# A two-layer encoder trunk in three-part fp32: x's second form split sooner, five of a pair's low parts by DMA, the last way down's buffers in another order, and PSUM tiles of two banks

## The chip, the cores and the metric

The kernel runs on one core of a Trainium2 chip. The time of a run is device microseconds for one launch. The time before is the median of three runs; the trace comes from one further, profiled execution. PE is TensorE, DVE VectorE, ACT ScalarE, POOL GpSimd, SP the engine that issues most loads.

## The reference

512 tokens of width 1024 go through two layers. Each layer is feed-forward, mixer, feed-forward, and a gated layer input, each with a residual and a layer norm:

```python
for i in range(DEPTH):                                   # DEPTH = 2
    x = layer_norm(A * x + 0.5 * swiglu_ffn(x, ffn1_wgu[i], ffn1_wd[i]), ...)
    x = layer_norm(A * x + (mlstm_mixer if i == 0 else gmlp_mixer)(x, ...), ...)
    x = layer_norm(A * x + 0.5 * swiglu_ffn(x, ffn2_wgu[i], ffn2_wd[i]), ...)
    ple = sigmoid(x @ ple_wg[i] + ple_bg[i]) * (p[i] @ ple_wp[i])
    x = layer_norm(A * x + ple, ...)

def swiglu_ffn(x, w_gu, w_d):                            # 1024 -> 2 x 2816 -> 1024
    g, u = split(x @ w_gu, 2)
    return (silu(g) * u) @ w_d
```

All is float32. The change touches the four feed-forward stages, and the places where a mixer or the gated input takes PSUM banks.

## The kernel before, in words

**Numbers in two parts.** A float32 operand is split into a high part (`whi`, `xh`: a ScalarE copy, L242) and a low part (`wlo`, `xl`: the rest, a VectorE subtraction, L251 or L257). `mm3` (L351 to L355) makes three matmuls of each product: high by high (L353), low by high (L354), high by low (L355).

**Weights.** `Weights` is one ordered list of (buffer kind, loads, make). `fill` takes it strictly in order: an entry is split as soon as a buffer of its kind is free, and the entries behind it wait for it. Kinds are `main` (4 buffers), `rows` (2 in a feed-forward stage) and `rowsx` (1, opened in the last pair at r = 2). Raw weights come by SP into 3 raw slots (`wraw`, 1 MB each) or smaller `wquarter` tiles; a slot is free when the last part made from it is done. A low part can also be made "by DMA": ScalarE writes the raw block negated, and rounded as the high part is, into `wlo` (L248), and POOL issues a transfer that adds the raw block to it (L249).

**A feed-forward stage** goes through the hidden columns in chunks of 2, 4, 4, 4, 4 and 4 blocks of 128. Chunks 0 to 3 make plain up products (`fps`, 24 matmuls of 512 columns each). Chunks 4 and 5 make them in pairs: seven products (`ups`, r = 0 to 6, 24 matmuls of 256 columns) give the gate and up blocks of two column blocks at once, after Strassen's scheme. There are four such pairs in a stage, 16 in the kernel. Their operands are sums of weight blocks and of x's quarters:

- weights (`up_forms`, L127): a11, a12, s2, s1, s3, s4, a22 for r = 0 to 6; s2 is formed in place on VectorE at L141 and L142, s3 at L149 and L150. `UP_BY_DMA` lists the r whose low part goes by DMA.
- x (`UpForms`, L950): plain quarters for r = 0, 1, 5; the forms t2 (`t_whi`, `t_wlo`) for r = 2, t1 (`t`) for r = 3, t3 for r = 4, t4 (`t_f`) for r = 6. They are made in chunk 3: from its third product on, two entries of `steps` follow each product. What is left is in `last`, which runs an entry after a product s of chunk 4 (there s = r in the first pair).

A product's result is taken by `UpPair.take`: ScalarE copies the bank after r = 0, 2 and 3 (L1047, `us<-ups`), and VectorE adds the bank to the copy after r = 1, 4 and 5 (L1050, L1052); `gate` is the Silu (L1061). Product r = 4 writes the bank that r = 2 filled, so it must wait for that copy. In `up_products` the order after each product is: product, `group.add`, `take`, the form's low part, the waiting low parts of weights, `formed.last`, release and fill, `gate`, forms of coming weights, and after every odd s a product of the way down.

**The way down** of chunk c is made during chunk c + 1 by a `Group`: seven products (`gps`, 12 matmuls of 512 columns) after the same scheme. A product fills two PSUM banks, which stay pinned, and `add` adds them to the residual `xt` by two VectorE instructions of 128x512 (L727). The last chunk's way down is plain (`down`, `dps`): four token blocks of 128, each over four row blocks of `wd`, into two banks; block t = 1 needs the second pair of banks, which the last `gps` products held until their adds. The order of that way down's weight buffers is a list, one for stages A and C, one for B and D, which end with the gated input (`ple`).

**PSUM for this** is a pool `ps_dn` of four single banks, handed out in turn by `dn_bank`; `turn_x` (transposes of x, `xps`), the mixers (`gvps`, `gps`) and the gated input (`pwp`) take banks from it as well.

The stages are A (first layer, before the mixer mlstm), B (first layer, after it, with ple), C (second layer, before the mixer gmlp) and D (after it, with ple).

Of the kernel before, what the change touches and what calls it, by code (L numbers as in the profile page):

```python
# [10 lines left out]
F32 = mybir.dt.float32  # L11
# [31 lines left out]
W_BUFS = 4  # L43
EXTRA = 2
PLE_EXTRA = 3
UP_BY_DMA = (1, 4, 5, 6)


class Weights:
# [273 lines left out]
def hybrid_trunk(ctx: ExitStack, tc, x, p, ln_g, ln_b, ffn1_wgu, ffn1_wd, ffn2_wgu, ffn2_wd,  # L323
# [18 lines left out]
    tmp = side_pool("tmp", 4, "right")  # L342
    small = side_pool("small", 4, "right")
    ps_up = ctx.enter_context(tc.tile_pool(name="ps_up", bufs=1, space=PSUM))
    ps_dn = ctx.enter_context(tc.tile_pool(name="ps_dn", bufs=1, space=PSUM))
    dram = ctx.enter_context(tc.tile_pool(name="dram", bufs=1, space=DRAM))

    mm = nc.tensor.matmul
# [29 lines left out]
        up_order.remove(i)  # L378
        up_order.append(i)

    dn_order, pinned = deque(range(4)), {}

    def dn_bank(name, pin=False):

        i = next(i for i in dn_order if i not in pinned.values())
        dn_order.remove(i)
        dn_order.append(i)
        bank = ps_dn.tile([P, 512], F32, name=name, tag=f"dn{i}")
        if pin:
            pinned[id(bank)] = i  # L390
        return bank

    def unpin(bank):
        i = pinned.pop(id(bank))
        dn_order.remove(i)
        dn_order.append(i)

# [43 lines left out]
    def ffn_weights(wgu, wd, name, ple=False):  # L441
        starts = [sum(FFN_CHUNKS[:c]) for c in range(LAST + 1)]

        def forms(c):
            m = FFN_CHUNKS[c] // 2

            def quarter(i, j):
                k = starts[c] + m * i
                return kp(wd)[:, k:k + m, j * 512:(j + 1) * 512]
            loads = [W.add_load(quarter(i, j), n, name) for i, j, n in ((0, 0, 2), (0, 1, 1), (1, 1, 1), (1, 0, 2))]  # L450
            return W.forms("rows", *((j, slice(None)) for j in loads))

        first = len(W.order)
        for at in range(starts[UP_FROM]):
            if at == 0 or at == starts[UP_FROM] - 1:
                W.add(*((kp(wgu)[:, :, c0:c0 + P], [slice(None)]) for c0 in (at * P, HID + at * P)))
            elif at % 2:
                add_pairs(wgu, at * P, HID + at * P)
        tiles = W.order[first:]
        del W.order[first:]  # L460
        for c, n in enumerate(FFN_CHUNKS):
            down_w = deque(forms(c - 1) if c else ())
            if c >= UP_FROM:
                products = []
                for b in range(starts[c], starts[c] + n, 2):
                    products += W.up_forms(*(W.add_load(kp(wgu)[:, :, c0:c0 + 2 * P], 2) for c0 in (b * P, HID + b * P)))
                for s, product in enumerate(products):
                    W.order.append(product)
                    if s % 2:
                        W.order.append(down_w.popleft())  # L470
                continue
            for i in range(2 * n):
                W.order.append(tiles[2 * starts[c] + i])
                if down_w:
                    W.order.append(down_w.popleft())
        if ple:
            W.add_hook("rows", lambda hi, lo: turn_p.pop()(hi, lo))
        add_rows(wd, starts[LAST], 4, ["rows", "rowsx", "main", "main"] if ple else ["main", "rows", "rows", "rowsx"])


    ML_SLOTS = (2, 3, 4, 5, 6, 7, 11)
# [271 lines left out]
    def down(hs, first, norm=None, lazy=False, defer=False):  # L753


        n = len(hs)
        ws, kinds = [], []

        def release(k):
            kind = kinds[k] if kinds[k].startswith("rows") else None  # L760
            if norm is None:
                W.release(kind=kind)
            elif kind:
                W.free[kind] += 1
            elif defer:
                W.release()
            else:
                W.release(later=lazy or bool(W.held))
                if not W.held:
                    W.held.append("none")  # L770

        for t in range(TB):
            banks = [dn_bank("dps"), dn_bank("dps")]
            for k in range(n):
                if k == len(ws):
                    ws.append(W.take())
                    kinds.append(W.kind)
                if norm is not None and k == 1 and t:
                    norm.prepare(t - 1)
                    if t >= 2:  # L780
                        turn_x(t - 2, up_bank, (0,), norm)
                        if not norm.deferred:
                            turn_x(t - 2, up_bank, (1,), norm)
                    norm.scale(t - 1)
                if norm is not None and k == 2 and t >= 2 and norm.deferred:
                    turn_x(t - 2, up_bank, (1,), norm)
                st = [a[:, t * P:(t + 1) * P] for a in hs[k]]
                for half, ps in enumerate(banks):
                    mv = [a[:, 0, half * 512:(half + 1) * 512] for a in ws[k]]
                    mm3(ps, st, mv, k == 0, k == n - 1)  # L790
                if t == TB - 1:

                    if norm is None or k > 2:
                        release(k)
                    elif k == 2:
                        for j in range(3):
                            release(j)

            def finish(t=t, banks=banks):
                for half, ps in enumerate(banks):  # L800
                    residual(t, half, ps, first)
                    if norm is not None:
                        norm.stats(t, half, 2)
                if norm is not None and t == TB - 1:
                    norm.apply(t)
                    set_hooks(norm)

            if defer and t == TB - 1:
                return finish
            finish()  # L810
            if first:
                run_affine()
# [51 lines left out]
    class Group:  # L864
# [58 lines left out]
        def product(self):  # L923
# [3 lines left out]
                self.finish_form()  # L927
            w, f = W.take(), self.ready.popleft()
            if r < 2:
                self.banks.append([dn_bank("gps", True) for _ in range(2)])  # L930
            for e, ps in enumerate(self.banks[r % 2]):
                for k in range(self.half):
                    i, j = (e, k) if self.by_tokens else (k, e)
                    mm3(ps, [a[:, i, j * P:(j + 1) * P] for a in f], [a[:, k] for a in w],
# [2 lines left out]
        def add(self):  # L937
# [3 lines left out]
                return  # L941
            self.next_add += 1
            i, j = self.TO[r]
            for e, ps in enumerate(self.banks[r % 2]):
                residual(2 * i + e, j, ps, r in self.first)
                if r >= 5:
                    unpin(ps)


    class UpForms:  # L950


        def __init__(self, pool, late):

            f32 = lambda at, tag: at.tile([P, 4, 256], F32, name="x_" + tag, tag=tag)
            a = [tmp.tile([P, 2, 256], F32, name="x_a", tag="pad", bufs=3) for _ in range(2)]
            b, c = f32(late, "wlo"), f32(pool, "f0")
            both = act.tile([P, 2, 4, 256], F32R, name="t1", tag="gb")
            self.t1, self.t2, self.t4 = [both[:, 0], both[:, 1]], [], []
            self.t3 = self.quarter(0, 1)  # L960
# [21 lines left out]
            def split_t1():  # L982
                for i, s in enumerate(halves):
                    split(self.t1[0][:, s], self.t1[1][:, s], a[i])

            self.steps = [
                x22, lambda: joined(b, 0, 1), t3, lambda: joined(c, 0, 0), lambda: vec.tensor_add(c, b, c),
                lambda: sca.activation(f32r(self.t2, late, "whi"), c, AF.Copy), t1, split_t1]

            d = [tmp.tile([P, 2, 256], F32, name="x_d", tag="pad", bufs=3) for _ in range(2)]  # L990

# [2 lines left out]
                    joined(d[i], 1, 0, s)  # L994

            def t4():
                hi = f32r(self.t4, pool, "f1")
                for i, s in enumerate(halves):
                    vec.tensor_sub(d[i], d[i], c[:, s])
                    sca.activation(hi[:, s], d[i], AF.Copy)  # L1000

            def t3_t2():
                split(*self.t3, b)
                vec.tensor_sub(f32r(self.t2, late, "wlo"), c, self.t2[0].bitcast(F32))

            def t4_low():
                lo = f32r(self.t4, pool, "f0")
# [1 line left out]
                    vec.tensor_sub(lo[:, s], d[i], self.t4[0][:, s].bitcast(F32))  # L1009

            self.steps += [x21, t4]
            self.last = {0: t3_t2, 3: t4_low}
            self.right = [self.quarter(0, 0), self.quarter(1, 0), self.t2, self.t1, self.t3,
                          self.quarter(1, 1), self.t4]

# [55 lines left out]
    def ffn(layer, k, rows, late, prepare=None):  # L1071
        with stage_pool("forms", 2) as fpool, stage_pool("quarters", Q_BUFS) as qpool, \
# [51 lines left out]
                return next_group if h is not None else None  # L1124

            for c, n in enumerate(FFN_CHUNKS):
                if c < LAST:
                    h = hpool.tile([P, 4, SEQ], F32, name="h", tag="h")[:, :n]
                elif prepare is not None:
                    prepare()  # L1130
# [61 lines left out]
    def mlstm():  # L1192
        b_in = ml_b_in
        with stage_pool("extra", EXTRA) as extra, stage_pool("ml_parts") as near, stage_pool("forms", 2) as fpool, \
# [11 lines left out]
                return a.rearrange("p a b -> p (a b)")  # L1206

            def gate_products():
                ps = dn_bank("gps")
                for kb in range(KB):  # L1210
                    st = gw[:, kb].rearrange("p e c -> p (e c)")
# [332 lines left out]
    def gmlp():  # L1544
        with stage_pool("extra", EXTRA) as extra, stage_pool("gm_parts") as near, stage_pool("ghpool") as hpool, \
# [54 lines left out]
            for c in range(4):  # L1600
# [8 lines left out]
                for t in range(TB):  # L1609
                    if t:  # L1610
                        run_hook()
                    if t == 1 and c < 3:
                        next_vb = load_bias(c + 1)
                    ps = dn_bank("gvps")
                    up_tokens(t, ws, ps, hook=run_hook if t else None, release=give_back)
                    dst = v_cols(c * 512, 512)[:, t]
# [146 lines left out]
    def ffn_ple(i, last):  # L1763
        with stage_pool("rows", 2) as rows, stage_pool("late") as late:
# [20 lines left out]
            with stage_pool("extra", PLE_EXTRA) as extra, stage_pool("rows2") as rows2, stage_pool("ple2") as mp:  # L1785
                W.open("extra", extra, PLE_EXTRA)
                W.open("rows2", rows2, 1)
                W.fill(2)
                finish()
                ph, pl = ph[0], pl[0]  # L1790
                bg = mp.tile([P, D], F32, name="bgb")
                sca.dma_start(bg, row_ap(ple_bg, i * D, D))
# [66 lines left out]
    def warm(n):  # L1859

        ps = up_bank("warm")
        for _ in range(n):
            nc.tensor.transpose(ps[:, :P], ident, ident)

    warm(16)
    turn_x(0)
    turn_x(1)
# [12 lines left out]
    ffn_stage(1, 0)  # L1880
    gmlp()
    ffn_ple(1, True)


# [25 lines left out]
```

## Time and profile before

| | |
|---|---|
| median of 3 runs | 2246.17 us (2243.39 to 2249.09) |
| profiled execution, its own time | 2251.26 us |
| span of its trace | 2249.5 us |
| mean granted TensorE clock | 0.994 |
| PE busy | 2207.3 us, 11669 matmuls |
| VectorE busy | 1693.8 us, 2452 instructions |
| ScalarE busy | 1059.5 us, 1492 instructions |
| POOL busy | 159.0 us, 199 instructions |
| low parts by DMA (L249) | 112 issues of 512 KB |

In a timeline row the columns are start (us from the span's start), duration (us), engine, line, operation, out<-in, shape; "xN" joins N instructions in a row, and the brackets give the idle time ahead of it and what ended it. In a row of waits they are the total in us, how often, and the longest. Instructions of VectorE and ScalarE overlap slightly, so that the distance of two starts is a little less than a duration.

### The profile page before, as it was taken

How to read it: one execution, taken by the hardware profiler on the slowest of the kernel's cores; microseconds unless marked ns; L12 is line 12 of the kernel's file. 1: busy time of each engine (PE TensorE's matmuls, PEld its weight loads, DVE VectorE, ACT ScalarE, POOL GpSimd, SP SyncE). 2: the span in 40 equal slices, each digit the busy share in tenths (PEclk: the TensorE clock that was granted, in tenths of full speed). 3: DMA queues.
4: the chain of work that ended last, by engine and by line, in shares of the span. 5: the costliest groups of instructions: out<-in, count | busy, mean ns of one | idle time of the engine just before them, and what ended most of it. 6: DMA issues, size and time to landing. Idle time of an engine off the chain costs nothing. (4 is left out here: it accounts for less than half of the span.)

```text
span 2249.5 us, 29438 instructions
## 1 busy us (share of the span) xinstructions
PE 2207.3 (98%) x11669; PEld 1896.6 (84%) x11669; DVE 1693.8 (75%) x2452; ACT 1059.5 (47%) x1492; POOL 159.0 (7%) x199
## 2 busy tenths in 40 slices
PE   9999999999999999999999999999999999999998
PEld 8888987888888888888888888987888888888877
DVE  5668787786776776688786768886788767678887
ACT  4334655464646433356444334655345453336542
POOL 1000110111101100001000000110001100001000
PEclk9999999999999999999999999999999999999999
DMA  6323754456847443246532333754437733335551
GB/s 200 104 93 113 179 137 131 108 143 133 155 123 155 126 131 94 93 121 161 169 122 66 115 101 112 178 135 137 140 76 151 168 122 113 103 113 124 139 168 57
DMA packets 215538, 287.31 MB, mean 128 GB/s; under 512 B 6836, under 2 KB 161588, under 8 KB 215400
## 3 DMA queue, kind: packets, MB, share of 16 engines
q1 hardware_dynamic: 168080, 211.83, 29.2%
q0 software_dynamic: 40704, 58.91, 16.4%
q10 hardware_dynamic: 6616, 14.69, 2.0%
q8 instruction: 92, 1.51, 0.3%
q14 instruction: 46, 0.38, 0.1%
HBM read 224.58 MB, written 2.11 MB: 101 GB/s over the span
## 5 line engine op out<-in xcount | busy, mean ns | idle before, releaser
L242 ACT ACTIVATE whi<-wraw 128x1024 fp32r<-128x1024 f32 (+1 forms) x388 | 400.0, 1047 | 247.8 <-DVE wraw L142 90.8
L353 PE MATMUL fps<-xh,whi 128*128 128x512 f32 x800 | 311.4, 389 | 0.0
L354 PE MATMUL fps<-xl,whi 128*128 128x512 f32 x800 | 311.2, 389 | 0.0
L355 PE MATMUL fps<-xh,wlo 128*128 128x512 f32 x800 | 311.2, 389 | 0.0
L251 DVE TENSOR_TENSOR wlo<-wraw,whi 128x1024 fp32r<-128x1024 f32 (+1 forms) x214 | 257.0, 1216 | 52.5 <-ACT whi L242 51.9
L353 PE MATMUL gps<-whi,fhi 128*128 128x512 f32 x644 | 251.9, 391 | 0.0
L354 PE MATMUL gps<-wlo,fhi 128*128 128x512 f32 x644 | 251.6, 391 | 0.0
L355 PE MATMUL gps<-whi,flo 128*128 128x512 f32 x644 | 251.3, 390 | 0.0
L242 ACT ACTIVATE whi<-wquarter 128x1024 fp32r<-128x1024 f32 (+1 forms) x140 | 135.6, 969 | 201.0 <-PE gps L355 132.8
L249 POOL DMA_DIRECT2D wlo<-wraw x112 | 114.2, 1020 | 1500.5 <-ACT wlo L248 1309.6
L251 DVE TENSOR_TENSOR wlo<-wquarter,whi 128x1024 fp32r<-128x1024 f32 (+1 forms) x92 | 97.6, 1061 | 160.6 <-ACT whi L242 160.6
L727 DVE TENSOR_TENSOR xt<-xt,gps 128x512 f32<-128x512 f32 x302 | 193.0, 680 | 1.2 <-PE gps L355 1.2
L355 PEld LDWEIGHTS fps<-xh,wlo 128*128 128x128 f32 x800 | 150.2, 188 | 31.3
L353 PEld LDWEIGHTS fps<-xh,whi 128*128 128x128 f32 x800 | 150.2, 188 | 31.1
L354 PEld LDWEIGHTS fps<-xl,whi 128*128 128x128 f32 x800 | 150.2, 188 | 30.9
L353 PE MATMUL ups<-xh,whi 128*128 128x256 f32 x512 | 147.6, 288 | 12.2 <-ACT us L1047 12.2
L355 PE MATMUL ups<-xh,wlo 128*128 128x256 f32 x512 | 147.5, 288 | 1.1 <-DMA wlo<-wraw 1.1
L354 PE MATMUL ups<-xl,whi 128*128 128x256 f32 x512 | 146.1, 285 | 0.0
L355 PEld LDWEIGHTS gps<-whi,flo 128*128 128x128 f32 x644 | 120.9, 188 | 26.2
L353 PEld LDWEIGHTS gps<-whi,fhi 128*128 128x128 f32 x644 | 121.1, 188 | 23.9
L354 PEld LDWEIGHTS gps<-wlo,fhi 128*128 128x128 f32 x644 | 121.1, 188 | 23.6
L905 ACT ACTIVATE fhi<-h 128x512 fp32r<-128x512 f32 (+1 forms) x140 | 80.8, 577 | 120.2 <-DVE h L1151 50.4
(361 smaller groups left out, 5056.5 us busy)
## 6 DMA issues: line engine op xcount, KB each, us to landing
wraw<-in_ffn_wgu_dram SPq DMA_DIRECT2D x79, 1024.0 KB, 7.3
wlo<-wraw POOLq DMA_DIRECT2D x112, 512.0 KB, 5.9
wquarter<-in_ffn_wd_dram SPq DMA_DIRECT2D x64, 512.0 KB, 3.8
wraw<-in_ml_w_in_dram SPq DMA_DIRECT2D x24, 1024.0 KB, 5.8
wraw<-in_gm_w_in_dram SPq DMA_DIRECT2D x15, 1024.0 KB, 5.6
wraw<-in_ffn_wgu_dram SPq DMA_DIRECT2D x17, 512.0 KB, 4.9
wraw<-in_ffn_wd_dram SPq DMA_DIRECT2D x8, 1024.0 KB, 6.3
wraw<-in_ml_w_out_dram SPq DMA_DIRECT2D x8, 1024.0 KB, 5.1
```

The source lines that it names most:

```text
L242: self.nc.scalar.activation(hi[:, s], src[:, s], AF.Copy)
L249: self.nc.gpsimd.dma_start(lo[:, s], src[:, s], accum_op=OP.add)
L251: self.nc.vector.tensor_sub(lo[:, s], src[:, s], hi[:, s].bitcast(F32))
L353: mm(ps, st[0], mv[0], start=start, stop=False, skip_group_check=more)
L354: mm(ps, st[0], mv[1], start=False, stop=False, skip_group_check=more)
L355: mm(ps, st[1], mv[0], start=False, stop=stop, skip_group_check=more)
L727: vec.tensor_add(dst, dst, ps)
L905: sca.activation(hi, src, AF.Copy)
```

## The change

It has four parts.

1. The low part of t2 is made in chunk 3, in the same step as its high part, and not after r = 0 of chunk 4. For that the buffer of `b` moves from `late`'s `wlo` to the forms' pool (`f1`). t4's two high copies move from the last step of chunk 3 to after r = 3 of chunk 4, and its low part from after r = 3 to after r = 4.
2. `UP_BY_DMA` gains r = 3, so that s1's low part is made by a ScalarE copy and a POOL transfer in place of a VectorE subtraction.
3. The last way down takes its buffers as `rowsx, rows, main, main` instead of `rows, rowsx, main, main` (B and D), and as `main, rows, rowsx, rows` instead of `main, rows, rows, rowsx` (A and C).
4. The way down's PSUM pool is now one of two tiles of two banks or of four tiles of one. `use_dn(2)` comes at chunk 1 of each feed-forward stage; `use_dn(1)` at the start, in `gate_products` of the first mixer, ahead of the third `gvps` product of the second, and after `finish` in the gated input. With two banks in a tile, a `Group` product is added to `xt` by one instruction of 1024 elements instead of two of 512.

```diff
-UP_BY_DMA = (1, 4, 5, 6)
+UP_BY_DMA = (1, 3, 4, 5, 6)
...
+    dn_order, pinned, dn = deque(), {}, {}
+
+    def use_dn(width):
+
+        if dn:
+            assert not pinned
+            dn["context"].__exit__(None, None, None)
+        dn["context"] = tc.tile_pool(name=f"ps_dn{width}", bufs=1, space=PSUM, reuse_waits="tile")
+        dn["pool"], dn["width"] = dn["context"].__enter__(), width
+        dn_order.clear()
+        dn_order.extend(range(4 // width))
+
+    def dn_tile(name, pin=False):
...
+        tile_i = dn["pool"].tile([P, dn["width"], 512], F32, name=name, tag=f"dn{i}")
...
-        add_rows(wd, starts[LAST], 4, ["rows", "rowsx", "main", "main"] if ple else ["main", "rows", "rows", "rowsx"])
+        add_rows(wd, starts[LAST], 4, ["rowsx", "rows", "main", "main"] if ple else ["main", "rows", "rowsx", "rows"])
...
-            banks = [dn_bank("dps"), dn_bank("dps")]
+            tiles = [dn_tile("dps") for _ in range(2 // dn["width"])]
+            banks = [tiles[0][:, half] if len(tiles) == 1 else tiles[half][:, 0] for half in range(2)]
...
-            for e, ps in enumerate(self.banks[r % 2]):
-                residual(2 * i + e, j, ps, r in self.first)
+            tiles = self.banks[r % 2]
+            for e, ps in enumerate(tiles):
+                n = 2 // len(tiles)
+                dst = xt[:, 2 * i + e:2 * i + e + n, j * 512:(j + 1) * 512]
+                if r in self.first:
+                    vec.scalar_tensor_tensor(dst, dst, ALPHA, ps, op0=OP.mult, op1=OP.add)
+                else:
+                    vec.tensor_add(dst, dst, ps)
                 if r >= 5:
                     unpin(ps)
...
-            b, c = f32(late, "wlo"), f32(pool, "f0")
+            b, c = f32(pool, "f1"), f32(pool, "f0")
...
+            def split_t2():
+                split(f32r(self.t2, late, "whi"), f32r(self.t2, late, "wlo"), c)
+
             self.steps = [
                 x22, lambda: joined(b, 0, 1), t3, lambda: joined(c, 0, 0), lambda: vec.tensor_add(c, b, c),
-                lambda: sca.activation(f32r(self.t2, late, "whi"), c, AF.Copy), t1, split_t1]
+                split_t2, t1, split_t1]
...
             def t4():
+                for i, s in enumerate(halves):
+                    vec.tensor_sub(d[i], d[i], c[:, s])
+
+            def t4_high():
                 hi = f32r(self.t4, pool, "f1")
                 for i, s in enumerate(halves):
-                    vec.tensor_sub(d[i], d[i], c[:, s])
                     sca.activation(hi[:, s], d[i], AF.Copy)
-
-            def t3_t2():
-                split(*self.t3, b)
-                vec.tensor_sub(f32r(self.t2, late, "wlo"), c, self.t2[0].bitcast(F32))
...
-            self.last = {0: t3_t2, 3: t4_low}
+            self.last = {0: lambda: split(*self.t3, b), 3: t4_high, 4: t4_low}
...
             for c, n in enumerate(FFN_CHUNKS):
+                if c == 1:
+                    use_dn(2)
...
             def gate_products():
+                use_dn(1)
                 ps = dn_bank("gps")
...
+                    if (c, t) == (0, 2):
+                        use_dn(1)
                     ps = dn_bank("gvps")
...
                 finish()
+                use_dn(1)
...
+    use_dn(1)
     warm(16)
```

More of the change, by code (lines that the diff above doesn't have):

```diff
@@ L344, in hybrid_trunk @@
     ps_up = ctx.enter_context(tc.tile_pool(name="ps_up", bufs=1, space=PSUM))
-    ps_dn = ctx.enter_context(tc.tile_pool(name="ps_dn", bufs=1, space=PSUM))
     dram = ctx.enter_context(tc.tile_pool(name="dram", bufs=1, space=DRAM))
@@ L379, in up_let_go @@
         up_order.append(i)
-    dn_order, pinned = deque(range(4)), {}
-    def dn_bank(name, pin=False):
+    dn_order, pinned, dn = deque(), {}, {}
[8 more added lines that the diff above has]
+    def dn_tile(name, pin=False):
         i = next(i for i in dn_order if i not in pinned.values())
@@ L387, in dn_bank, with unpin @@
         dn_order.append(i)
-        bank = ps_dn.tile([P, 512], F32, name=name, tag=f"dn{i}")
+        tile_i = dn["pool"].tile([P, dn["width"], 512], F32, name=name, tag=f"dn{i}")
         if pin:
[L390 to L394, printed above, removed]
+            pinned[id(tile_i)] = i
+        return tile_i
+    def dn_bank(name):
+        return dn_tile(name)[:, 0]
+    def unpin(tile_i):
+        i = pinned.pop(id(tile_i))
         dn_order.remove(i)
@@ L929, in product @@
             if r < 2:
-                self.banks.append([dn_bank("gps", True) for _ in range(2)])
-            for e, ps in enumerate(self.banks[r % 2]):
+                self.banks.append([dn_tile("gps", True) for _ in range(2 // dn["width"])])
+            for e in range(2):
+                tiles = self.banks[r % 2]
+                ps = tiles[0][:, e] if len(tiles) == 1 else tiles[e][:, 0]
                 for k in range(self.half):
@@ L943, in add @@
             i, j = self.TO[r]
-            for e, ps in enumerate(self.banks[r % 2]):
-                residual(2 * i + e, j, ps, r in self.first)
+            tiles = self.banks[r % 2]
+            for e, ps in enumerate(tiles):
[5 more added lines that the diff above has]
+                    vec.tensor_add(dst, dst, ps)
                 if r >= 5:
@@ L1882, in hybrid_trunk @@
     ffn_ple(1, True)
+    dn["context"].__exit__(None, None, None)
 _INS = ['x', 'p', 'ln_g', 'ln_b', 'ffn1_wgu', 'ffn1_wd', 'ffn2_wgu', 'ffn2_wd',
```

## The prediction

> **What bounds the kernel now.** I read the page first, then the chain of waits of the matmul engine, then the windows of the stretches in which those waits fall, and then the timeline around each wait.
>
> ```profile
> span 2249.5 us, 29438 instructions
> PE 2207.3 (98%) x11669; PEld 1896.6 (84%) x11669; DVE 1693.8 (75%) x2452; ACT 1059.5 (47%) x1492; POOL 159.0 (7%) x199
> PE ups L353 <- ACT us L1047: 12.2, 12, 2.5
> PE dps L353 <- DVE xt L727: 7.0, 3, 3.5
> PE ups L354 <- DVE t_wlo L1004: 5.1, 4, 1.3
> PE dps L353 <- ACT whi L242: 2.4, 2, 1.2
> PE ups L355 <- DMA wlo<-wraw: 2.2, 3, 1.1
> PE dps L354 <- DVE wlo L257: 1.5, 2, 0.8
> 212.00:340.00 128.00, 123.47 (x847) 114.60 (x847) 106.33 (x129) 75.92 (x97) 12.64 (x15) 0.99 0.60 146
> 348.00:350.00 2.00, 1.54 (x4) 1.25 (x5) 1.97 (x4) 0.00 (x0) 0.00 (x0) 0.50 1.03 389
> 350.00:352.00 2.00, 2.00 (x6) 1.56 (x5) 1.90 (x5) 0.00 (x0) 0.00 (x0) 0.50 0.17 62
> 1528.00:1532.00 4.00, 3.51 (x9) 2.83 (x10) 3.86 (x8) 0.00 (x0) 0.00 (x0) 0.57 0.83 307
> 2159.00:2164.00 5.00, 5.00 (x17) 3.94 (x16) 5.00 (x6) 2.75 (x3) 0.00 (x0) 0.66 0.69 225
> ```
>
> The first two lines are the page's: TensorE works for 98% of the span, and the change takes no product from it, so only its waits can be won. The six wait lines (total us, times, longest) sum to 30.4 us. The last five are windows (us, then busy time of PE, weight load, DVE, ACT, POOL, then granted clock, DMA share, GB/s). 212 to 340 is the paired part (chunks 4 and 5) of the first feed-forward stage: VectorE is busy for 106.33 of 128 us (83%) there. The others are the ends of the first, third and fourth stage, where the clock was 0.50, 0.57 and 0.66; I call the stages A, B, C, D.
>
> **Part 1: t2's split sooner.** Each stage loses one wait of up to 1.3 us on t2's low part.
>
> ```profile
> 221.53 1.23 DVE L1004 TENSOR_TENSOR t_wlo<-x_f,t_whi 128x1024 fp32r<-128x1024 f32 x1
> 222.81 0.38 PE L354 MATMUL ups<-t_wlo,whi 128*128 128x256 f32 x1 [1.29 <-DVE t_wlo L1004]
> 201.54 1.23 DVE L251 TENSOR_TENSOR wlo<-wquarter,whi 128x1024 fp32r<-128x1024 f32 x1 [2.18 <-ACT whi L242]
> 213.21 1.24 ACT L1000 ACTIVATE t_f<-x_d 128x512 fp32r<-128x512 f32 x2 [3.10 <-DVE x_d L999]
> 235.25 1.29 DVE L1009 TENSOR_TENSOR t_f<-x_d,t_f 128x512 fp32r<-128x512 f32 x2
> 237.65 0.68 DVE L1052 TENSOR_TENSOR us<-us,ups 128x512 f32<-128x512 f32 x1
> 240.48 0.28 PE L353 MATMUL ups<-t_f,whi 128*128 128x256 f32 x1
> ```
>
> The matmul of 222.81 starts as the subtraction ends. In chunk 3, where the subtraction goes, VectorE idles 2.18 us at 201.54, more than the 1.23 it needs, so I cost it at nothing there; without that cover, at 1.23. The gain is the whole wait line, -5.1 (bounds -5.1 and 0: 0 if another low of r=2 is as late). t4's high copies (1.24 of ScalarE at 213.21) move to after r=3, where ScalarE is the less busy engine: nothing, at worst 1.24 per stage ahead of a bank copy. t4's low (L1009) leaves r=3 for r=4, behind that step's work on VectorE. Without it, L1052 starts 1.2 sooner, at about 236.4; then come L1052, a form's low part and two sums (four of 512 elements, 0.6 to 0.65 each as in L1009's 1.29 for two) and a weight's low (1.15 by the next rows), 3.6 in all. So the moved one starts at 240.0 and its halves end at 240.65 and 241.2, against a PE that wanted the first at 240.6, its second matmul, where before it lay ready at 236.5. I take 0.35 late in each stage, +1.4 (bounds 0, and 4.8 if the whole 1.2 is late in each of four).
>
> **Part 2: five low parts by DMA.** The third entry of 16 pairs leaves VectorE and costs one ScalarE copy and one POOL issue.
>
> ```profile
> 252.25 1.23 DVE L150 TENSOR_TENSOR wraw<-wraw 128x1024 f32<-128x1024 f32 x1
> 253.57 1.06 ACT L242 ACTIVATE whi<-wraw 128x1024 fp32r<-128x1024 f32 x1 [4.05 <-DVE wraw L150]
> 273.74 1.23 DVE L141 TENSOR_TENSOR wraw<-wraw 128x1024 f32<-128x1024 f32 x1 [6.84 <-DMA wraw<-in_ffn_wgu_dram]
> 1108.44 6.90 DVE L257 TENSOR_TENSOR wlo<-wraw,whi 128x1024 fp32r<-128x1024 f32 x6 [1.30 <-ACT whi L242]
> 291.75 0.63 ACT L1061 ACTIVATE us<-us 128x512 f32<-128x512 f32 x1 [3.09 <-DVE us L1050]
> 293.76 0.57 ACT L1047 ACTIVATE us<-ups 128x512 f32<-128x512 f32 x1
> 294.38 0.39 PE L353 MATMUL ups<-xh,whi 128*128 128x256 f32 x1 [2.37 <-ACT us L1047]
> ```
>
> Read upwards from 294.38: PE waits for the bank copy L1047, the copy stands in ScalarE's queue behind L1061, and L1061 waited 3.09 us for VectorE's L1050. So the 12.2 us are VectorE's lateness seen through ScalarE. VectorE lost it at 273.74, where it stood 6.84 us for a raw load; that load could only go out when a low part of the pair before had landed, whose chain begins with L150 at 252.25 and ScalarE at 253.57, which had been idle 4.05 us. The removed low is 1.15 per pair (six in a row take 6.90 at 1108.44); t2's low and t4's copies take another 1.2 to 2.4 from the first pair. Ahead of the copy of 293.76 VectorE is thus 2.3 to 3.6 sooner, against a wait of 2.37. The added copy (0.94 by the next rows) falls into the idle 3 to 4 us ahead of 253.57 and 291.75. In the fourth pair of B and D it stands before the copy of r=0, about 0.2 each. I take 2.0 of the 12.2 as left, -10.2 (bounds: 12.2 all gone; or all left, should ScalarE itself be late).
>
> ```profile
> L249 POOL DMA_DIRECT2D wlo<-wraw x15: 828/846/852, 227.5 to 327.1; - x15
> DMA to landing us min/median/max: 4.5/5.4/9.5
> 1077.47 1.04 ACT L242 ACTIVATE whi<-wraw 128x1024 fp32r<-128x1024 f32 x1
> 1078.41 0.58 ACT L1047 ACTIVATE us<-ups 128x512 f32<-128x512 f32 x1
> 1085.80 0.28 PE L355 MATMUL ups<-t,wlo 128*128 128x256 f32 x1
> ```
>
> The new transfer must land between the high part of r=3 and its first use: 1077.47 to 1085.80, 8.3 us in this tightest pair, some 9.5 in others. It needs two copies (0.94 each, from the start of 1077.47 to that of 1078.41), 0.3 to issue and 5.4 to land: 7.6, so it is hidden with 0.7 us to spare; at the 9.5 of the slowest landing it is 3.4 late. POOL is queued 0.85 more per pair with r=4's issue behind it, 12.64 busy of 128: nothing. The present DMA wait of 2.2 gains what VectorE gains before it; I take 0.7 left, -1.5 (bounds -2.2 and +3).
>
> **Part 3: the order of the last way down.**
>
> ```profile
> 1115.26 1.27 DVE L727 TENSOR_TENSOR xt<-xt,gps 128x512 f32<-128x512 f32 x2
> 345.49 1.06 ACT L242 ACTIVATE whi<-wraw 128x1024 fp32r<-128x1024 f32 x1 [1.09 <-DMA wraw<-in_ml_w_in_dram]
> 348.46 0.80 PE L353 MATMUL dps<-whi,wquarter 128*128 128x512 f32 x1 [3.48 <-DVE xt L727]
> ```
>
> B and D: the first entry takes the buffer that is free early, so the waits of 1.2 and 0.8 go. But the next token block waits for L727 behind the six lows of 1108.44: they become five (-1.15), the add +0.54 until its second half is done (next part), so what is won early is waited for there. Net -0.6 and -1.0, -1.6 (bounds -3.9, the two wait lines, and 0). A and C: the end waits for a transfer (345.49) before the last low, so one low fewer does nothing: 0 (bounds -1.1 and +1.1 each, a low more or less in front).
>
> **Part 4: PSUM tiles of two banks.**
>
> ```profile
> 287.45 1.28 DVE L727 TENSOR_TENSOR xt<-xt,gps 128x512 f32<-128x512 f32 x2
> 288.65 1.22 DVE L111 TENSOR_TENSOR wquarter<-wquarter 128x1024 f32<-128x1024 f32 x1
> 1554.08 0.48 PE L353 MATMUL gvps<-whi,xh 128*128 128x512 f32 x1
> 1554.85 0.68 DVE L1617 TENSOR_TENSOR gvf<-gvps,gvb 128x512 f32<-128x512 f32 x1
> 1560.95 0.68 DVE L1617 TENSOR_TENSOR gvf<-gvps,gvb 128x512 f32<-128x512 f32 x1
> ```
>
> Two adds take 1.20 (287.45 to 288.65); one of 1024 elements, which the trace lacks with a PSUM operand, I take near the 1.15 of the lows, also of 1024 elements, at 1.14: -0.06 times 140 products is -8 us of VectorE, none of it on PE's path by itself (bounds 1.0 and 1.28 an add). The Trainium skill, "VectorE: DVE Perf Modes", section on the TRN2 errata, says that a VectorE instruction pays a fixed term of some 150 cycles, and gives 0.96 GHz; an estimate by that page is 0.157 each, 22 us of VectorE. By it t4's low would not be late either and the sum below would be -14.2; by the row it is -12.8, and I keep the row.
>
> On the path: at the ends of A and C PE is released by the add, which ends at 1.22 instead of the first half's 0.68: +0.54 each, +1.1 (bounds 0 and 1.3). With two tiles instead of four banks the second `gvps` product, begun at 1554.08, has to wait for the add of 1554.85 to end at 1555.53: +1.5; the turn of x before the third waits for L1617 of 1560.95, +0.9. The mixer of the first layer +0.2, B's `pwp` +0.5, by the same 0.68 add. In all +3.1 (bounds 0, where the work behind has slack, and 4.5).
>
> **Sum.** -5.1 +1.4 -10.2 -1.5 -1.6 +1.1 +3.1 = -12.8. The profiled execution took 2251.26 (span 2249.5), 5.09 above the median 2246.17; 2251.26 - 12.8 = 2238.5 profiled, and 5.1 below it the median: 2233.4. The three runs lie 5.7 us apart; 0.3% (6.7 us) is about what can be told from no change.
>
> The cold clock stays in this sum: 348 to 352 ran at 0.50 after a wait of 3.48, and 2159 to 2164 at 0.66 where the waits were only 1.2 and 0.8. The Trainium skill, "TensorE: Matmul & The Clock Gate", Part 1 (the HAM clock gate), has the clock halved after an idle window of about 3.4 us. A's wait agrees, D's does not; by that rule D's cold clock (a third of 5 us, 1.7 lost) would have to vanish as its waits shrink, and the sum would be -14.5.
>
> **Rivals.** (1) No real gain, 2245: ScalarE, not VectorE, is what makes the copy late, since it gains 0.95 per pair. Then -10.2 and -1.5 fall away: -1.1. For it: 2.0 us pass in ScalarE's own queue between the starts of L1061 and L1047. Against: the 3.09 and 4.05 us it idled for VectorE just before. (2) Slower, 2268: the new low of r=3 lands late. The place is L355 of r=3, the point an average landing of 8.1 us: 0.8 late in each of 16 pairs eats the 12.8; slower by 0.3% from 8.5; at 9.5, 2.2 late on average, 35 us less 12.8, and +22. For it: max 9.5, and a queue that gets 25% more. Against: the median 5.4. (3) More gain, 2224: VectorE comes to the ends of A and C so much sooner that the 7.0 waited for L727 shrinks to 1.1 and the cold clock (4 us at 0.50 lose 2.0 at A; 0.43 of the some 3.3 us that PE works at C lose 1.4) goes: -9.3 more. Against: 345.49 waits for a transfer, not for VectorE.
>
> **Numbers.** Main case 0.60 (own range 2227 to 2240), rival 1 0.20, rival 2 0.08, rival 3 0.12. The range 2224 to 2246 leaves out half of rivals 1 and 3 and all of 2, 0.2 or a little more. Faster than 2239.4: rival 3 and nearly all of the main case, 0.70; slower than 2252.9: 0.08; the same 0.22.
>
> **What would show it.** The wait on t_wlo gone; L1047's line at about 2; a new wait on t_f's low of r=6 of 0.3 in the first pair; waits before `gvps` of 1.5; L355 on the DMA under 1; POOL issues of wlo 112 to 128, VectorE 28 us less busy (16 x 1.2 and 8), ScalarE 15 more. It goes wrong if L1047's line stays (ScalarE late), if L355 waits for the DMA in most pairs, or if the ends' L727 waits change by more than 1 us.

## The result, and the profile after

| | before | changed |
|---|---|---|
| median (8 runs each) | 2246.19 us | 2235.78 us (2233.61 to 2243.31) |
| ratio to before, 95% interval | | 0.9961 (0.9945 to 0.9977) |
| the same kernel in a second series of 8 (25 of before) | 2246.68 us | 2238.99 us, ratio 0.9966 (0.9953 to 0.9979) |
| profiled execution, its own time | 2251.26 us | 2243.31 us |

The kernel is 10.4 us faster by the medians of the first series and 7.7 by those of the second (forecast 12.8); the ratios' intervals stand for 5.2 to 12.4 and 4.7 to 10.6 us. One of the twelve executions of x_t4 (below) took 5668.59 us, with no cause on record, and is left out of its ratio. The trace after is of an execution at the upper end of its runs, 7.5 us above the median, as the trace before was 5.1 above its own. So the two traces alone differ by 7.9 us of span, and a second trace was taken (below).

Line numbers have moved: `mm3` is L352 to L354 now, the way down's adds to `xt` are L966 (in a `Group`; L727 before) and L739 (the plain way down), the bank copy is L1070, t4's low part L1032. The first two lines of the page after, and the matmul engine's waits (total us, times, longest):

```profile
span 2241.6 us, 29337 instructions
PE 2203.8 (98%) x11669; PEld 1894.0 (84%) x11669; DVE 1668.4 (74%) x2296; ACT 1074.6 (48%) x1508; POOL 172.6 (8%) x215
PE dps L352 <- DVE xt L966: 9.5, 4, 3.5
PE ups L354 <- DMA wlo<-wraw: 6.2, 4, 2.4
PE ups L352 <- ACT us L1070: 3.8, 5, 1.1
PE ups L353 <- DVE t_f L1032: 2.5, 4, 0.6
PE dps L353 <- DVE wlo L257: 1.5, 2, 0.8
PE gps L352 <- ACT fhi L918: 1.3, 1, 1.3
PE gvps L352 <- DVE gvf L1645: 1.3, 1, 1.3
PE xps L607 <- DVE gvf L1645: 0.8, 1, 0.8
```

The wait on t2's low part (5.1) is gone, the bank copy's (L1047 before, L1070 now) fell from 12.2 to 3.8, and the wait of 2.4 on a high part at the ends of B and D is gone. Six lines are new or larger: t4's low part 2.5, the mixer's start 1.3 and 0.8, one wait of 1.3 on a ScalarE copy (L918) in stage C, the ends 7.0 to 9.5, and the transfers of low parts 2.2 to 6.2. The 1.5 on a low part at the ends of B and D is as before. VectorE is busy 25.4 us less, ScalarE 15.1 more, POOL 13.6 more.

In the timeline, the late low part of t4 in stage A, one wide add with the instruction behind it, and the mixer's start:

```profile
238.54 1.28 DVE L1032 TENSOR_TENSOR t_f<-x_d,t_f 128x512 fp32r<-128x512 f32 x2
239.28 0.39 PE L353 MATMUL ups<-t_f,whi 128*128 128x256 f32 x1 [0.61 <-DVE t_f L1032]
250.69 1.21 DVE L966 TENSOR_TENSOR xt<-xt,gps 128x1024 f32<-128x1024 f32 x1
251.82 0.68 DVE L1073 TENSOR_TENSOR us<-us,ups 128x512 f32<-128x512 f32 x1
1551.45 0.50 PE L352 MATMUL gvps<-whi,xh 128*128 128x512 f32 x1 [1.27 <-DVE gvf L1645]
1558.50 0.66 PE L607 MATMUL xps<-ident,xt 128*128 128x128 f32 x4 [0.82 <-DVE gvf L1645]
```

Here the first half of L1032 ends at 239.2 and PE goes on at 239.28; the add of 1024 elements lets the next instruction start after 1.13 us; both waits of the mixer are for the `gvf` add, as worked out.

### The profile page after: what moved, and what is told of

The parts are those of the page before. It is cut to its first block, busy times and chain, and to the rows that moved or that the text cites. A ratio compares the mean times of both kernels' runs of the same rounds, so it can differ in the third digit from the quotient of the medians.

```text
span 2241.6 us, 29337 instructions
## 1 busy us (share of the span) xinstructions
PE 2203.8 (98%) x11669; PEld 1894.0 (84%) x11669; DVE 1668.4 (74%) x2296; ACT 1074.6 (48%) x1508; POOL 172.6 (8%) x215
## 4 chain that ended last, share of the span: by engine, by line
PE 80%; DVE 8%; ACT 5%; issue 3%; DMA 3%; POOL 0%; ACTq 0%; DVEq 0%; POOLq 0%; SPq 0%
PE fps L352 7%; PE fps L354 7%; PE fps L353 7%; PE gps L354 6%; PE gps L352 6%; PE gps L353 6%; PE ups L354 2%; PE ups L353 2%; PE ups L352 2%; PE dps L352 2%; PE dps L353 2%; PE dps L354 2%; DMA wlo<-wraw 2%; ACT whi L242 2%; DVE wlo L257 1%
## 5 line engine op out<-in xcount | busy, mean ns | idle before, releaser
L352 PE MATMUL fps<-xh,whi 128*128 128x512 f32 x800 | 311.4, 389 | 0.0
L354 PE MATMUL fps<-xh,wlo 128*128 128x512 f32 x800 | 311.2, 389 | 0.0
L251 DVE TENSOR_TENSOR wlo<-wraw,whi 128x1024 fp32r<-128x1024 f32 (+1 forms) x210 | 252.2, 1216 | 51.7 <-ACT whi L242 50.9
L352 PE MATMUL gps<-whi,fhi 128*128 128x512 f32 x644 | 252.0, 391 | 1.3 <-ACT fhi L918 1.3
L354 PE MATMUL gps<-whi,flo 128*128 128x512 f32 x644 | 251.3, 390 | 0.0
L249 POOL DMA_DIRECT2D wlo<-wraw x128 | 127.8, 1000 | 1474.8 <-ACT wlo L248 1311.0
L966 DVE TENSOR_TENSOR xt<-xt,gps 128x1024 f32<-128x1024 f32 (+1 forms) x178 | 185.1, 1051 | 2.1 <-PE gps L354 2.0
L354 PEld LDWEIGHTS fps<-xh,wlo 128*128 128x128 f32 x800 | 150.2, 188 | 31.2
L352 PEld LDWEIGHTS fps<-xh,whi 128*128 128x128 f32 x800 | 150.2, 188 | 31.0
L352 PE MATMUL ups<-xh,whi 128*128 128x256 f32 x512 | 145.4, 284 | 3.3 <-ACT us L1070 3.2
L354 PE MATMUL ups<-xh,wlo 128*128 128x256 f32 x512 | 145.2, 284 | 1.5 <-DMA wlo<-wraw 1.5
L354 PEld LDWEIGHTS gps<-whi,flo 128*128 128x128 f32 x644 | 120.9, 188 | 26.6 <-DVE flo L921 0.4
L352 PEld LDWEIGHTS gps<-whi,fhi 128*128 128x128 f32 x644 | 121.1, 188 | 25.4 <-ACT fhi L918 1.5
L921 DVE TENSOR_TENSOR flo<-h,fhi 128x512 fp32r<-128x512 f32 (+1 forms) x140 | 88.8, 635 | 67.7 <-ACT fhi L918 66.9
```

Of the source, the lines that this page charges most:

```text
L249: self.nc.gpsimd.dma_start(lo[:, s], src[:, s], accum_op=OP.add)
L251: self.nc.vector.tensor_sub(lo[:, s], src[:, s], hi[:, s].bitcast(F32))
L352: mm(ps, st[0], mv[0], start=start, stop=False, skip_group_check=more)
L354: mm(ps, st[1], mv[0], start=False, stop=stop, skip_group_check=more)
L921: vec.tensor_sub(lo, src, hi.bitcast(F32))
L966: vec.tensor_add(dst, dst, ps)
```

## The experiments

All were timed against the kernel before; a ratio has its 95% interval. The changed kernel stands at 0.9961 and 0.9966. "Changed" edits are against the changed kernel.

**again: the changed kernel once more.**

> The changed kernel once more, for a second trace. Its eight times fall into two groups: five from 2233.6 to 2235.8 us and three from 2242.4 to 2243.3, and the trace at hand is of 2243.31. Theory 1 (collision): the 8.5 us between the groups are one or two accumulating transfers of the paired part that run beside a 1 MB raw load, take 9 to 10 us instead of 4.5 to 5.5, and make VectorE and ScalarE late in the third pair of stage C (waits of 1.46, 0.72, 1.26, 2.53 and 1.20 us there, 7.2 together). If this trace is of the lower group, those waits are gone and the DMA line of 6.2 us is under 3. Theory 2 (clock): the groups differ in the clock around the ends of the stages. Then the waits of the third pair stand as before and the cold stretches differ by some 8 us of matmul time.

Ratio 0.9966, median 2238.99; the trace has a span of 2236.1 us, 5.5 less than the first. In it the transfers' line is 2.0, the copy's 4.5 and the ends' 10.2. The same program differs most in the third pair of stage C. First the earlier trace, then this one; SP issues two 1 MB raw loads, POOL a low part, and VectorE's L141 waits for one of these loads:

```profile
1437.34 0.86 POOL L249 DMA_DIRECT2D wlo<-wraw  x1 [4.20 <-ACT wlo L248]
1437.43 2.81 SPq L208 DMA_DIRECT2D wraw<-in_ffn_wgu_dram  x2
1447.90 1.23 DVE L141 TENSOR_TENSOR wraw<-wraw 128x1024 f32<-128x1024 f32 x1 [10.84 <-DMA wraw<-in_ffn_wgu_dram]
1453.35 0.50 PE L352 MATMUL gps<-whi,fhi 128*128 128x512 f32 x1 [1.30 <-ACT fhi L918]
```

```profile
1436.07 2.84 SPq L208 DMA_DIRECT2D wraw<-in_ffn_wgu_dram  x2
1437.12 0.86 POOL L249 DMA_DIRECT2D wlo<-wraw  x1 [3.95 <-ACT wlo L248]
1442.21 1.23 DVE L141 TENSOR_TENSOR wraw<-wraw 128x1024 f32<-128x1024 f32 x1 [5.12 <-DMA wraw<-in_ffn_wgu_dram]
```

In the second execution the loads go out 1.05 us ahead of the low part, and L141 starts at 1442.21; in the first they go out 0.09 behind it, that transfer takes 10.2 us instead of 7.7, the first load lands after 10.4 us instead of 6.0, and L141 starts 5.7 us later, with a run of waits behind it. The loads went out after another low part had landed, 7.9 us after its issue instead of 6.5. So these two traces fit the theory of meeting transfers. But the moment of issue does not settle the landing alone. In stage B, a low part issued 0.84 us behind a raw load in both traces landed after 9.1 us in the first and 7.7 in the second, and PE waited 2.31 and 0.92 us for it. That meetings make the two groups of times is not shown: this series lay between the groups, and no trace of the lower one was taken. The recorded clocks leave a smaller share for theory 2: their mean is 0.9960 in the three executions of the upper group and 0.9972 in the five of the lower, by PE's 2204 us an estimated 2 to 3 of the 8.5 us.

**u_dma: r = 3 by VectorE again.**

```diff
-UP_BY_DMA = (1, 3, 4, 5, 6)
+UP_BY_DMA = (1, 4, 5, 6)
```

> The changed kernel with r = 3 taken out of the list of low parts by DMA again. If VectorE's lateness set the bank copy (the prediction's step of -10.2), most of it comes back: the L1070 line from 3.8 to 8 or more, and the median is 5 to 9 us above the changed kernel's, some 2242. If the t2 split alone freed VectorE (rival), the median stays at 2235 to 2237 and, with 16 transfers fewer, the DMA line falls from 6.2 towards 2.

Ratio 0.9977 (0.9967 to 0.9987), 2241.33 us. Its waits:

```profile
PE ups L352 <- ACT us L1070: 8.0, 6, 1.6
PE ups L353 <- DVE t_f L1032: 4.8, 4, 1.2
PE ups L354 <- DMA wlo<-wraw: 0.3, 1, 0.3
```

The copy's line came back to 8.0 as expected, and t4's rose to 4.8; the transfers' line went to 0.3. The transfer of r = 3 is thus worth 2.3 to 5.5 us by the medians; the intervals overlap, so this run alone does not show it.

**u_banks: single banks throughout.** All calls of `use_dn` but the first are taken out.

```diff
-                if c == 1:
-                    use_dn(2)
```

> The changed kernel with four single banks throughout, so two adds of 512 per product again. Theory: the 2.1 us of waits at the gmlp mixer's start go (gvps 1.3 and xps 0.8), the ends of A and C gain 0.5 each, and VectorE is 8 to 10 us busier, which costs at most 2 in the paired part: the median is 1 to 3 us below the changed kernel's, 2233 to 2235. Rival: VectorE's 8 us matter in the paired part (139 adds ahead of bank adds and low parts); then the median is 2 or more above, 2238 to 2242, with the L1070 line back above 6.

Ratio 0.9923 (0.9905 to 0.9940), 2231.20 us: 4.6 and 7.8 us below the two medians of the changed kernel, more than expected. The interval lies below both of the changed kernel's. VectorE is busier again (1675.2 us). The copy's line is 5.8, above the 3.8 and 4.5 with two banks, but two later runs show it the other way round (3.2 in b_t43, 6.0 in x_t43), so no worth of the wide add can be told from it. No wait stands at the mixer's start, where the two took 2.1. The waits of B's and D's ends are 1.04 and 1.08 instead of 1.50 and 1.49; those of A and C, 3.32 and 3.27, are not to be told from the changed kernel's (3.46 and 3.09, again 4.08 and 3.10):

```profile
PE dps L352 <- DVE xt L966: 8.7, 4, 3.3
PE ups L352 <- ACT us L1070: 5.8, 7, 1.3
PE ups L354 <- DMA wlo<-wraw: 0.9, 1, 0.9
```

**u_forms: x's forms as before.**

```diff
-            self.last = {0: lambda: split(*self.t3, b), 3: t4_high, 4: t4_low}
+            self.last = {0: t3_t2, 3: t4_low}
```

> The changed kernel with x's forms as before: t2's low part after r = 0, t4's high copies in chunk 3 and its low part after r = 3. Theory: the waits on t2's low part come back at 1.3 us in each stage (5.1), those on t4's low part go (2.5 in the wait line): the median is 3 to 6 us above the changed kernel's, 2239 to 2242. Rival: with r = 3's low part off VectorE the subtraction of t2 is early enough anyway; then nothing comes back and the median is 0 to 3 below, 2233 to 2236.

Ratio 0.9996 (0.9985 to 1.0008): nothing is left of the gain. Not only does the wait on t2's low part come back (3.0 here), the copy's line is higher too; the transfers' line lies between those of the two traces of the changed kernel (6.2 and 2.0):

```profile
PE ups L352 <- ACT us L1071: 6.4, 10, 1.3
PE ups L354 <- DMA wlo<-wraw: 5.4, 6, 1.8
PE ups L353 <- DVE t_wlo L1028: 3.0, 4, 0.7
```

**u_order: the last way down's buffers as before.**

```diff
-["rowsx", "rows", "main", "main"] if ple else ["main", "rows", "rowsx", "rows"]
+["rows", "rowsx", "main", "main"] if ple else ["main", "rows", "rows", "rowsx"]
```

> The changed kernel with the last way down's buffers in their old order in all four stages. Theory: at B and D the wait of 1.2 us on the high part of the first row block comes back and the later wait on L966 falls from 1.65 to about 1; at A and C the end is bound by the next stage's transfer and nothing moves. The median is 0.5 to 2 us above the changed kernel's (two series of eight gave 2235.8 and 2239.0), and the cold stretch at the end of D (clock 0.66 before, gone after) comes back. Rival: the order at A and C is what delays their ends (the 0.3 us wait on a low part that is new in C); then the median is 1 to 2 below and the L966 line falls under 9.

Ratio 0.9969 (0.9957 to 0.9981), 2238.43 us: not to be told from the changed kernel. The wait on the high part comes back at B and D, and the later waits shrink: D's on L966 is gone, B's is 1.30.

```profile
PE dps L352 <- DVE xt L966: 8.7, 3, 3.7
PE dps L352 <- ACT whi L242: 2.4, 2, 1.2
2140.00:2165.00 25.00, 23.70 (x104) 19.26 (x105) 23.68 (x36) 8.74 (x12) 1.59 (x3) 0.93 0.35 126
```

The window holds D's end, at a clock of 0.93 as before the change (below).

**x_t4: both parts of t4 one product sooner.**

```diff
-            self.last = {0: lambda: split(*self.t3, b), 3: t4_high, 4: t4_low}
+            self.last = {0: lambda: split(*self.t3, b), 2: t4_high, 3: t4_low}
```

> The changed kernel with t4's two parts one product sooner: high copies after r = 2, low part after r = 3. Theory: the wait on t4's low part (2.4 to 2.5 us by the wait line, 0.77 in each stage by the distance of two matmuls, 3.1) goes and nothing takes its place, since t2's low part stays in chunk 3: the median is 2 to 3 us below the changed kernel's. Rival: the subtraction then stands ahead of the bank add after r = 4 and of r = 5's sums as it did before the change, and the wait comes back as one on L1070 or on a low part of r = 4 or 5; then the median stays within 1 us.

Ratio 0.9982 (0.9972 to 0.9993), 2242.86 us: 4 to 7 us slower than the changed kernel. The wait on t4's low part went, and the transfers' line rose to 8.9. The cause stands in the timeline of the first pair. The changed kernel, with the landing time of that transfer (us, from the view of the tile `wlo`):

```profile
230.65 0.83 POOL L249 DMA_DIRECT2D wlo<-wraw  x1 [3.52 <-ACT wlo L248]
231.84 0.37 SPq L208 DMA_DIRECT2D wraw<-in_ffn_wgu_dram  x1
DMA to landing us min/median/max: 5.5/5.5/5.5
```

And this one:

```profile
PE ups L354 <- DMA wlo<-wraw: 8.9, 8, 2.5
231.60 0.83 POOL L249 DMA_DIRECT2D wlo<-wraw  x1 [4.56 <-ACT wlo L248]
231.74 0.37 SPq L208 DMA_DIRECT2D wraw<-in_ffn_wgu_dram  x1
DMA to landing us min/median/max: 8.6/8.6/8.6
240.20 0.39 PE L354 MATMUL ups<-t_f,wlo 128*128 128x256 f32 x1 [1.52 <-DMA wlo<-wraw]
```

The two high copies moved ahead of the low part's negated copy in ScalarE's queue. The issue moved by 0.95 us, from 1.19 ahead of the raw load to 0.14 ahead of it, and the transfer took 3.1 us longer. Neither theory had said this. Of the line of 8.9, 8.2 are at r = 6.

**x_rot: single banks from the mixer's first product on.**

```diff
-                    if (c, t) == (0, 2):
+                    if (c, t) == (0, 0):
                         use_dn(1)
+                        dn_order.rotate(-2)
```

> The changed kernel with single banks from the first gvps product of the second mixer on, handed out beginning with the third bank, so that the two-bank tiles stay for the feed-forward stages alone. Theory: the waits at the mixer's start (gvps 1.3 and xps 0.8, 2.4 us by the distance of two matmuls) go, and the median is 2 to 2.5 us below the changed kernel's; of the 5 to 8 us that single banks throughout gave, the rest then lies at the ends of the stages. Rival: the whole gain of the single banks is at this start; then this kernel reaches 2231 too.

Ratio 0.9973 (0.9962 to 0.9983), 2238.01 us; a miss. The rotation handed out the banks of the last token block, so the mixer's waits of 1.3 and 0.8 became one of 4.0 on that block's adds, and the question of the mixer's share stayed open:

```profile
PE gvps L352 <- DVE xt L739: 4.0, 1, 4.0
```

**b1: single banks and t4 as in x_t4.**

> Single banks throughout and t4's parts one product sooner; the DMA list and the buffer order as changed. If the two gains are apart (theory), 2231.2 less 3 us: 2227 to 2230, with neither a wait on t4's low part nor one on gvps. If both are the same slack of VectorE (rival: with two adds of 512 per product VectorE is late for the moved subtraction's successors), the median stays at 2230 to 2233.

Ratio 0.9973 (0.9962 to 0.9984), 2239.28 us, 8 above u_banks. The gains do not add, but not by VectorE's slack as the rival had it. The waits on transfers are back, 8.3 of them at r = 6, and in the first pair the low part's issue is again level with a raw load (232.00 against 232.17):

```profile
PE ups L354 <- DMA wlo<-wraw: 8.5, 6, 2.4
```

**x_t43: only t4's low part sooner.**

```diff
-            self.last = {0: lambda: split(*self.t3, b), 3: t4_high, 4: t4_low}
+            self.last = {0: lambda: split(*self.t3, b), 3: lambda: (t4_high(), t4_low())}
```

> The changed kernel with t4's low part directly behind its high copies, after r = 3, and those copies where the change put them. In the kernel that had both one product sooner the two copies stood ahead of r = 6's low part by DMA in ScalarE's queue: its issue moved from 230.65 to 231.60, level with the raw load of 231.74, the transfer took 8.55 us instead of 5.52, and L354 of r = 6 waited 1.68. Theory (transfers that meet): here the issue stays at about 230.6, the landing at about 5.5 us, the wait on t4's low part (0.77 in each stage) goes and no wait on the transfer comes: 2 to 3 us below the changed kernel's, 2233 to 2236. Rival: VectorE's order alone counts, and a subtraction after r = 3 makes the following ones late whatever ScalarE does; then the first pair's r = 6 waits 1.5 to 2.5 again and the median is near 2242.

Ratio 0.9958 (0.9945 to 0.9972). The wait on t4's low part is gone and the transfers' line is 2.7. In the first pair the low part is issued 1.18 us ahead of the raw load again and lands after 5.5, so what had hurt there in x_t4 was ScalarE's order. But against the changed kernel no gain can be told (forecast 2 to 3 us): the copy's line is 6.0 in this trace.

```profile
PE ups L352 <- ACT us L1070: 6.0, 8, 1.4
PE ups L354 <- DMA wlo<-wraw: 2.7, 3, 1.8
230.78 0.83 POOL L249 DMA_DIRECT2D wlo<-wraw  x1 [3.52 <-ACT wlo L248]
231.96 0.37 SPq L208 DMA_DIRECT2D wraw<-in_ffn_wgu_dram  x1
```

**b_t43: the same with single banks.**

> The same with single banks throughout. If the two gains are apart (theory): 2231.2 less 2 to 3 us, 2228 to 2230, the lowest so far. If t4's low part one product sooner hurts as it did with the high copies sooner too (2239.3, rival), it stays above 2236.

Ratio 0.9910 (0.9894 to 0.9926), 2227.64 us (2223.14 to 2231.44): the fastest, 8 to 11 us below the changed kernel by the medians, and its interval lies wholly below the changed kernel's. Against u_banks (0.9923) the intervals overlap.

```profile
PE dps L352 <- DVE xt L966: 7.8, 4, 3.1
PE ups L352 <- ACT us L1070: 3.2, 3, 1.2
PE ups L354 <- DMA wlo<-wraw: 2.8, 2, 2.4
```

**f_only: the first part alone** (x's forms; the DMA list and the order as before, four single banks). It is built from the changed kernel, so the rewritten pool stays, with the setting `reuse_waits="tile"` that `ps_dn` did not have; that was not run apart. u_forms has it too, with two-bank tiles, and gained nothing.

> The kernel before with the first part alone (t2's split in chunk 3, t4's parts later): DMA list, buffer order and single banks as before. The prediction's own terms for it: the wait on t2's low part gone (-5.1), t4's late (+1.4), and VectorE 1.2 to 2.4 us sooner in the first pair, of which the copy line gets perhaps 2: 2240 to 2242. Theory after the runs so far (r = 3 by DMA gives little beside it, and the two-bank tiles cost 5): this part is most of the gain, some 8 to 10 us, 2236 to 2238.

Ratio 0.9961 (0.9947 to 0.9975), 2239.30 us: by itself it gives what the whole change gives, 8.8 us by the medians of its own series, nearer to the later theory (8 to 10) than to the prediction's terms (4 to 6).

```profile
PE ups L352 <- ACT us L1070: 7.4, 6, 1.7
PE ups L353 <- DVE t_f L1032: 5.6, 4, 1.4
```

**b_t43_dma4: the fastest with r = 3 by VectorE.** The edit of u_dma in b_t43.

> The fastest so far (single banks throughout, t4's low part directly behind its high copies after r = 3; 2227.64 us, ratio 0.9910) with r = 3's low part on VectorE again. If that transfer pays by taking 16 subtractions off VectorE (theory), the copy line L1070 goes from 3.2 to 7 or 8 us, the line of waits on transfers from 2.8 to near 0, and the ratio is 0.993 to 0.994, 4 to 6 us slower. Rival: what it takes from the copies it gives back in transfers that land late; then the ratio stays within 0.9900 to 0.9925.

Ratio 0.9943 (0.9927 to 0.9959), 2233.60 us. The copy's line is 7.7 against 3.2, the transfers' 0.2 against 2.8; the two intervals just part. The transfer of r = 3 pays, by about 6 us by the medians and 7 by the ratios.

## Why the prediction was right, and where not

The time was forecast at 2233.4 and came at 2235.78 and 2238.99, within its range. The gain of 12.8 lies a little above both intervals. And not all of the gain is waits, as the sum had it. PE's idle time (span less busy) was 42.2 us before and 37.8 and 34.3 in the two traces after, 4.4 and 7.9 less. Its busy time for the same 11669 matmuls fell by 3.5 and 5.5, at a mean granted clock of 0.994 before and 0.996 in both traces after. The sum had left the clock as it was, so part of the nearness is luck. The trace before ran at a lower clock than most executions of its kernel: the means are 0.9959 over 25 of them and 0.9968 over the second series of the changed kernel, 0.0009 more. An estimate from that and PE's 2204 us is 2 us for the clock, of a gain of 8 to 10.

The terms of the sum, from the waits after:

- **t2's low part, -5.1**: gone in all four stages, as said.
- **t4's low part, +1.4**: 2.5 by the wait line (2.4 in the second trace). The place was right, the size too small: 0.61 in each stage where 0.35 was taken, and 1.39 in f_only, where VectorE still makes r = 3's low part.
- **The bank copy, -10.2**: -8.4 in the first trace (12.2 to 3.8), -7.7 in the second (4.5). The size was too large. The reading that VectorE's lateness is seen through ScalarE held: f_only brought the line to 7.4, and taking r = 3's subtraction off VectorE brought it from 8.0 to 3.8 (u_dma) and from 7.7 to 3.2 (b_t43_dma4), though ScalarE is 15 us busier for it. Rival 1 falls.
- **The wait on transfers, -1.5**: this step failed. It became 6.2 in one trace and 2.0 in the other. I had looked for lateness at r = 3, where the trace after shows none; 4.7 of the 6.2 came at r = 6 (waits of up to 2.4 there), and in the second trace 0.9 of 2.0. What the step left out is that a low part can land later when a raw load runs beside it (x_t4: 8.6 us instead of 5.5). Rival 2 named the right resource at the wrong place, and its price was partly paid.
- **The order, -1.6**: this failed in part. The waits of 1.2 on the high part went at B and D, but those of 0.8 on the low part stayed (the line of 1.5 is the same before and after), and the later waits on the add rose from 0.77 to 1.50 at B and from none to 1.49 at D: -0.2 in all, and nothing of it can be told in the time.
- **The ends of A and C, +1.1, and the mixer's start, +3.1**: the mixer's two waits came at 1.27 and 0.82 (forecast 1.5 and 0.9); the 0.7 for the first mixer and `pwp` stands in no wait line. A and C went from 3.48 and 2.79 to 3.46 and 3.09 (again 4.08 and 3.10), +0.3 to +0.9. The ends' line rose by 2.5 in all, most of it at B and D, more than the 1 us that the prediction named as a sign of being wrong. Rival 3, which had it shrink to 1.1, falls. Undoing the banks gave back 4.6 to 7.8 by the medians, more than the waits found for them (2.1 at the mixer, 0.9 at B and D); where the rest lies is open.
- **The wide add**: 1.13 against the 1.14 taken; no effect on the path can be told of the 7 us that VectorE was spared (1675.2 in u_banks, 1668.4 here).

So the time was near and the division of the sum was not. I had put 3.7 us on the first part as such and 9.1 on the other three with the copy's line; f_only and u_forms show that the first part carries all of the net gain, 8.8 us where I had put 3.7. The transfer of r = 3 gains 2 to 6 us, the two-bank tiles cost 5 to 8, and the order does nothing that can be measured. The mixer's share of the banks' cost was not measured apart, since x_rot missed.

On the clock, which the prediction left standing at 0.50 to 0.66 at the ends: the first three are windows of 25 us over D's end before, after and in f_only, the last one of 5 us in the second trace after (the third figure from the end is the clock).

```profile
2140.00:2165.00 25.00, 22.63 (x127) 19.49 (x128) 16.75 (x21) 12.99 (x17) 1.36 (x2) 0.93 0.78 232
2140.00:2165.00 25.00, 22.76 (x128) 19.20 (x127) 20.99 (x28) 8.78 (x11) 0.93 (x1) 1.00 0.67 243
2140.00:2165.00 25.00, 22.19 (x101) 17.54 (x100) 22.72 (x34) 7.52 (x9) 1.48 (x2) 1.00 0.46 170
2127.00:2132.00 5.00, 4.74 (x25) 4.65 (x26) 2.07 (x3) 2.50 (x4) 0.85 (x1) 0.66 1.02 184
```

u_order and f_only have the same old order of buffers and the same line of 2.4 on the high part, and one ran D's end at 0.93, the other at 1.00. So the cold stretch comes and goes with the same waits, and its absence at D's end after is not shown to be the order's doing. In the second trace of the changed kernel such a stretch stands in D's last pair, at 0.66 behind waits of 0.47 and 1.05 us. The ends of A and C stayed cold: 344 to 348 and 1522 to 1530 both ran at 0.57 after. The Trainium skill, "TensorE: Matmul & The Clock Gate", Part 1 (the HAM clock gate), calls the window in which the engine's activity is watched free-running, so that it matters where in it the matmuls fall. u_order and f_only fit that; they do not show it.

## What to carry to other kernels

In this kernel a subtraction moved into a stretch where its engine had time paid more than the wait that it removed (8.8 us for the first part, against a wait line of 5.1), since the same engine's lateness stood behind a second, larger wait on another engine, which fell from 12.2 to 7.4. Before merging two instructions, ask which wait the saved time stands behind: 140 wider adds saved 7 us of VectorE time with no gain that could be told, and the coarser buffers that they needed cost 5 to 8 us. An instruction put ahead of a transfer's issue can cost more than its own length, if the issue slides onto another transfer. And before a sum of waits is compared with a gain, compare busy time and clock of the two traces.

## What the runs showed of the hardware that was not expected

A 512 KB accumulating transfer landed in 5.5 us when issued 1.19 us ahead of a raw load (after) and in 8.6 when issued 0.14 ahead of it (x_t4). In one and the same program, two raw loads issued one behind the other and the accumulating transfer beside them held L141 for 10.84 us in one execution and for 5.12 in another; the loads had moved by 1.4 us. A transfer issued 0.84 us behind a load in both of these executions landed after 9.1 and 7.7 us. The spans of the two differ by 5.5 us, a quarter of a per cent.

The granted clock fell to 0.66 over 5 us behind two waits of 1.2 and 0.8 us (before, D's end) and behind two of 0.47 and 1.05 (again), and stayed at 1.00 behind waits of 1.2 and 0.8 in f_only.
